# A hybrid decoder block on one core: B's Gram products and key transposes in a fixed order over both PSUM banks

## The chip, the core and the metric

The kernel runs on one core of a Trainium2 chip. The metric is the device time of one execution in microseconds (us). A core has several engines that work side by side, each through its own queue of instructions in order: TensorE (PE; it loads weights, PEld, and multiplies, PE), VectorE (DVE), ScalarE (ACT), GpSimd (POOL) and SyncE (SP), which here issues nearly all DMAs. PE writes its products into PSUM, which is divided into banks; DVE and ACT read them from there into SBUF, the working memory.

## What is computed

The input is 1024 tokens of width 1024, with 16 learned meta tokens put in front. One layer does three things: a half-step SwiGLU feed-forward, a pair of mixers whose outputs are gated and merged, and another half-step SwiGLU. The change lies in the mixers:

```python
u = _rmsnorm(h, mix_norm[l])
aq, ak, av, az, abeta, aalpha, bcols, ga, gb = jnp.split(u @ w_in[l], ...)
o_a = _deltanet_branch(aq, ak, av, az, abeta, aalpha, ...)   # A: chunked gated DeltaNet, 8 heads of 128
o_b = _rwkv7_branch(bcols, ...)                              # B: RWKV-7 time mixing, 16 heads of 64
merged = jax.nn.sigmoid(ga) * o_a + jax.nn.sigmoid(gb) * o_b
h = h + merged @ w_out[l]
```

Mixer B is a recurrence over tokens, for each head with a 64 x 64 state:

```python
def step(state, inp):
    r_t, w_t, k_t, v_t, a_t, b_t = inp
    sa = jnp.einsum('bhvk,bhk->bhv', state, a_t)
    state = state * w_t[:, :, None, :] + sa[..., None] * b_t[:, :, None, :] \
        + v_t[..., None] * k_t[:, :, None, :]
    return state, jnp.einsum('bhvk,bhk->bhv', state, r_t)
```

The kernel computes it in chunks of 64 tokens. Within a chunk it needs the products of the chunk's keys with its queries (the Gram products), the inverse of a triangular matrix made from them, and the keys transposed.

## The kernel before

**Stages.** The first feed-forward runs from 0 to about 730 us of the profiled execution, the mixers (`middle`) from there to about 2260 us, then the output projection and the second feed-forward. The tokens are in two segments: the first has 512 tokens and the 16 meta tokens, the second the other 512. `middle` runs 16 iterations, numbered 0 to 15: for each segment the eight values of `j`, and each iteration handles one head of A and two heads of B, which lie in the lower and the upper 64 partitions (`HS[0]`, `HS[1]`).

**Pipelining.** A list written out by hand (`schedule()`, with the strings `REGULAR`, `SWITCH` and others) says in which order the actions of neighbouring iterations are written: `merge_blocks` and `transitions` of the current iteration, then `operands` and `inverses` of the next one, `chains` and `gates` of the current, `finish`, then `decay`, `new_b` and `new_a` of the one after the next.

**What sets the order on an engine.** The functions write instructions, and a scheduler in the tile framework puts those of each engine into one fixed order when the kernel is built, by when it reckons that their inputs and their memory are ready, and else by the order in which they were written. It also sets the waits. So neighbouring instructions of the source may be far apart on PE, with instructions of other actions between them. `g.tc.issue_after(ins)` says that what is traced under it on the engine of `ins` comes somewhere behind `ins`. Before the change only `chains` uses it.

**PSUM.** In `middle` eight banks are shared out: two for `ch` (merge_blocks, transitions, chains), and for the rest `main_banks(g, 2, 2)` gives four to the projections (`pp`) and two to `mx`, from which all small products of `operands`, `new_b` and others come. At the step `banks`, near the end of the first segment, `main_banks(g, 1, 3)` makes that three and three.

**The Gram products (L1428).** `operands` takes the eight chunks of its two heads in two groups of four (`c4`). For each group it takes two `mx` tiles `ps[0]` and `ps[1]`, a bank each. For a chunk there are four products: `h` picks the lower or upper 64 partitions to read (64 rows of the array), `d` the bank, and `h ^ d` the 64 partitions of the bank that are written (64 columns of the array). Thus each of the four products of a chunk uses another quarter of the array: `d` = 0 the two quarters on the diagonal, into bank 0; `d` = 1 the other two, into bank 1. Each has 128 columns to stream. DVE then reads each bank, masks it and writes `LT` (L1431), bank 0 first.

**What follows from LT.** `inverse_inputs` sends the diagonal 32 x 32 blocks of LT to a buffer in HBM (`scr`) with eight DMAs on SP (L1548), then four of A's matrix `UA` (L1551), and reads it all back as `Ub` (L1557). `inverses` then runs 31 steps on DVE, two instructions each (`tb` L1581, `Xb` L1583), and its result comes back by DMA for the next iteration's `merge_blocks`. In `new_b` a product named `bon` (a sum over channels, L1213) follows a row of DVE instructions.

**The key transposes (L1498).** Further down in `operands`, two `mx` tiles `ps` take the transposed keys and b vectors of all eight chunks: again four products for a chunk, with `d` and `h` as above, here against an identity, 64 columns each. ACT copies both banks into `BKt` (L1501), which the next `transitions` needs.

Of the kernel before, what the change touches and what calls it, by code (L numbers as in the profile page):

```python
# [13 lines left out]
P = 128  # L14
# [12 lines left out]
CB = 64  # L27
# [6 lines left out]
HS = (slice(0, 64), slice(64, 128))  # L34
# [1018 lines left out]
def ch3(ap, c):  # L1053
    return ap.rearrange("p (a b) -> p a b", b=c)
# [189 lines left out]
def key(i, h):  # L1244

    return 1 - tok(i, h)


def run(g, pool, name, *kinds):


    ps, out, used = {}, [], [0, 0]
    for f in kinds:
        ds = [f(i, 0)[2] ^ f(i, 0)[3] for i in range(2)]
        at = []
        for d in ds:
            if d not in ps:
                ps[d] = pool.tile([P, 512], F32, name=name, tag=pool.name)
            at.append(used[d])
            used[d] += NCB // 2 * CB  # L1260
        for i in range(NCB):
            e, c0 = ds[i & 1], at[i & 1] + i // 2 * CB
            for h in range(2):
                l, r, src, dst = f(i, h)
                assert src ^ dst == e
                g.nc.tensor.matmul(ps[e][HS[dst], c0 : c0 + CB], lhsT=l, rhs=r, start=True, stop=True)  # L1266
        out.append([(ch3(ps[d][:, c0 : c0 + NCB // 2 * CB], CB), cs) for d, c0, cs in zip(ds, at, EO)])
    return out
# [50 lines left out]
def new_b(g, q):  # L1319
# [12 lines left out]
    for ps, cs in run(g, g.mx, "vbp", lambda i, h: (v[HS[h], off + i * CB : off + (i + 1) * CB],  # L1332
                                                    g.C("cmat")[HS[h], HS[h]], h, key(i, h)))[0]:
        nc.scalar.activation(Vs[:, cs], ps, AF.Copy)
# [76 lines left out]
def operands(g, q):  # L1411

    nc, st, V, c, j, n, off = g.nc, g.st, g.V, q.c, q.j, q.n, q.off
# [3 lines left out]
    kq, AR, BK = q.kq, q.AR, q.BK  # L1417
# [2 lines left out]


    LT = q.LT = st.tile([P, NCB, 2, P], F32, name="LT", tag="LT", bufs=2)
    for c4 in range(0, NCB, 4):
        ps = [g.mx.tile([P, 512], F32, name="grb", tag="mx") for _ in range(2)]
        for i in range(4):
            for d in range(2):
                for h in range(2):
                    nc.tensor.matmul(ps[d][HS[h ^ d], i * P : (i + 1) * P], lhsT=BK[HS[h], c4 + i, d ^ (i & 1)],  # L1428
                                     rhs=AR[HS[h], c4 + i].rearrange("p a b -> p (a b)"), start=True, stop=True)
        for d in range(2):  # L1430
            nc.vector.tensor_tensor(LT[:, c4 : c4 + 4, d], ch3(ps[d], P),  # L1431
                                    g.C("mB").unsqueeze(1).to_broadcast([P, 4, P]), op=ALU.mult)
    if meta:
        nc.vector.tensor_copy(g.bkpm[0:64, 0, :], g.bkm[0:64, :])
        nc.vector.tensor_copy(g.bkpm[64:128, 1, :], g.bkm[64:128, :])
        ps = g.mx.tile([P, 512], F32, name="gbm", tag="mx")
# [25 lines left out]
    for b in range(2):  # L1462
        ps = g.mx.tile([P, 512], F32, name="gra", tag="mx")
        for c2 in range(2):
            i = 2 * b + c2
            tsl = slice(off + i * CA, off + (i + 1) * CA)
            nc.tensor.matmul(ps[:, c2 * 256 : c2 * 256 + 256], lhsT=kq[:, 0, tsl], rhs=kq[:, :, tsl],  # L1467
                             start=True, stop=True)
# [23 lines left out]
    BKt = q.BKt = st.tile([P, NCB, 2, CB], F32, name="BKt", tag="BKt")  # L1492
    ident = g.C("ident")
    ps = [g.mx.tile([P, 512], F32, name="bkt", tag="mx") for _ in range(2)]
    for i in range(NCB):
        for d in range(2):
            for h in range(2):
                nc.tensor.matmul(ps[d][HS[h ^ d], i * CB : (i + 1) * CB], lhsT=BK[HS[h], i, d ^ (i & 1)],  # L1498
                                 rhs=ident[HS[h], HS[h]], start=True, stop=True)
    for d in range(2):  # L1500
        nc.scalar.activation(BKt[:, :, d], ch3(ps[d], CB), AF.Copy)  # L1501

# [4 lines left out]
    def vr(i, h):  # L1507
        k = key(i, h)
        return Vs[HS[k], i], LT[HS[k], i, 1 - (i & 1), CB:], k, h

    pa, pr = run(g, g.mx, "vp", lambda i, h: (AR[HS[h], i, 0, :], ident[HS[h], HS[h]], h, tok(i, h)), vr)
    for ps, cs in pa:
        nc.scalar.activation(at[:, cs], ps, AF.Copy)
    for ps, cs in pr:
        nc.scalar.activation(ch3(yb, CB)[:, cs], ps, AF.Copy)
    if meta:
        btm = q.btm = st.tile([64, P], F32, name="btm", tag="btm", bufs=2)
        ps = g.mx.tile([P, 512], F32, name="btp", tag="mx")
# [3 lines left out]
    ps = g.mx.tile([P, 512], F32, name="ktp", tag="mx")  # L1522
# [3 lines left out]
    if meta:  # L1526
        vkm = q.vkm
        ps = g.mx.tile([P, 512], F32, name="vmp", tag="mx")
# [11 lines left out]
def inverse_inputs(g, q):  # L1540
# [4 lines left out]
    for b in range(4):  # L1545
        sl, lo = slice(32 * b, 32 * b + 32), 32 * (b % 2)
        for e, cs in enumerate(EO):
            nc.sync.dma_start(sv[b][:, cs], q.LT[sl, cs, e, lo : lo + 32])  # L1548
    for b in range(4):
# [55 lines left out]
def merge_blocks(g, q):  # L1605

    nc, st = g.nc, g.st
    LT, UA, Xc, XA = q.LT, q.UA, q.Xc, g.XA
    Y = g.Y[q.it % 2]
# [3 lines left out]
    for t in range(NT):  # L1613
        for o in (0, 64):
            u12 = LT[o : o + 32, t, t & 1, 32:64] if t < NCB else UA[o : o + 32, t - NCB, o + 32 : o + 64]
            nc.tensor.matmul(ps[o + 32 : o + 64, t * 32 : t * 32 + 32], lhsT=u12, rhs=nat(Xc[o : o + 32, t]),
# [28 lines left out]
def transitions(g, q):  # L1645

    nc, st = g.nc, g.st
    Y = g.Y[q.it % 2]
    AR, LT, BKt, Vs, yb = q.AR, q.LT, q.BKt, q.Vs, ch3(q.yb, CB)
    vbk = q.vbk = st.tile([P, NCB, CB], F32, name="vbk", tag="vbk")  # L1650
# [20 lines left out]
    def vb(i, h):  # L1671
        k = key(i, h)
        return BKt[HS[k], i, 1 - (i & 1)], Vs[HS[k], i], k, h

    px, pv = run(g, g.ch, "xp", solved(q.at), va)
    for ps, cs in pv:
        nc.scalar.activation(vka[:, cs], ps, AF.Copy)
# [130 lines left out]
def finish(g, q):  # L1808
# [17 lines left out]
    else:  # L1826
        g.mg.append(u_tile(g, yb))


ACTIONS = {"new_b": new_b, "tokens": tokens, "new_a": new_a, "operands": operands, "inverses": inverses, "merge_blocks": merge_blocks, "transitions": transitions,  # L1830
           "chains": chains,
           "gates": gates, "finish": finish, "fill": fill}
# [86 lines left out]
```

## Time and profile before

| | |
|---|---|
| median of three runs | 3012.78 us (3006.31 to 3014.66) |
| profiled execution, its own time | 3009.62 us |
| its span, first to last instruction | 3007.6 us |
| PE busy | 2890.0 us (96%) |
| DVE busy | 2194.8 us (73%) |
| mean granted PE clock | 0.99 |
| busy on Gram products (L1428), 1024 records | 60.77 us of PE |
| busy on key transposes (L1498), 1024 records | 29.81 us of PE |

The profile is one execution. Its page has the busy time of each engine, the chain of work that ended last, and groups of instructions; the trace behind it answers by line, by window and as a timeline. A timeline row has the start and the length of a run of like instructions in us, engine, line, operation, output and inputs, shapes and the count, and in brackets how long the engine was idle before it and what ended that. A run's length goes to the end of its last instruction, and runs on PE overlap where products of different quarters do.

### The profile page before, as it was taken

The page shows a single profiled execution, that of the slowest core. Times are in us where ns is not written, and L with a number is a line of the kernel's source. Part 1 is how long each engine was busy: PE and PEld are TensorE (multiplying, and loading weights), DVE is VectorE, ACT ScalarE, POOL GpSimd, SP SyncE. Part 2 cuts the span into 40 slices and gives each one's busy share as a digit, 9 for nine tenths or more (in the row PEclk, how much of TensorE's full clock was granted, in tenths as well). Part 3 has the DMA queues.
Part 4 walks back from the last instruction along what each step waited for, and adds up shares of the span by engine and source line. Part 5 has one row for each costly group of instructions (what it writes and reads, how often), then busy time and mean ns, then how long its engine had stood idle before and what let it go on. Part 6 is the DMA issues. An engine that isn't in the chain of part 4 may idle for free.

```text
span 3007.6 us, 62829 instructions
## 1 busy us (share of the span) xinstructions
PE 2890.0 (96%) x25630; PEld 2501.7 (83%) x25630; DVE 2194.8 (73%) x4079; ACT 1445.0 (48%) x2546; POOL 491.2 (16%) x554
## 2 busy tenths in 40 slices
PE   8999999998989999999998999999998999999998
PEld 8999999998878888888776777777776888888886
DVE  7566668776667877788767887777866666667886
ACT  5322234345655656566566656656644432223444
POOL 0332332323000000000000100100100033332531
PEclk9999999999999999999999999999999999999999
DMA  3433236453232322333332332233354333333762
GB/s 123 134 107 106 93 122 210 170 193 111 74 74 66 83 72 64 81 82 87 93 90 71 81 82 75 74 84 86 106 148 158 114 109 103 100 104 132 248 226 95
DMA packets 286849, 333.14 MB, mean 111 GB/s; under 512 B 172432, under 2 KB 178576, under 8 KB 286560
## 3 DMA queue, kind: packets, MB, share of 16 engines
q1 hardware_dynamic: 284752, 325.77, 35.7%
q8 instruction: 201, 3.29, 0.5%
q10 hardware_dynamic: 1728, 3.16, 0.3%
q14 instruction: 88, 0.72, 0.1%
q0 software_dynamic: 80, 0.19, 0.0%
HBM read 261.67 MB, written 67.38 MB: 109 GB/s over the span
## 4 chain that ended last, share of the span: by engine, by line
PE 50%; DVE 12%; ACT 5%; issue 2%; DMA 1%; SPq 0%; POOL 0%; DVEq 0%; ACTq 0%
PE pp L307 16%; PE pg L494 11%; PE pd L707 6%; PE pwo L307 3%; DVE w L164 2%; DVE tb L1581 1%; PE pg L518 1%; DVE Xb L1583 1%; ACT w L163 1%; PE cs L1213 1%; PE vp L1266 1%; PE mp L1266 1%; DVE mt L1689 1%; PE gra L1467 1%; PE np L1266 1%
## 5 line engine op out<-in xcount | busy, mean ns | idle before, releaser
L307 PE MATMUL pp<-uk,w 128*128 128x512 f32 (+2 forms) x4824 | 969.8, 347 | 15.2 <-DVE h L714 6.0
L307 PEld LDWEIGHTS pp<-uk,w 128*128 128x128 f32 x4824 | 744.0, 191 | 111.9 <-DVE w L164 13.1
L707 PE MATMUL pd<-form,w 128*128 128x256 f32 (+2 forms) x2772 | 437.2, 320 | 9.9 <-DVE w L164 9.2
L707 PEld LDWEIGHTS pd<-form,w 128*128 128x128 f32 x2772 | 396.7, 190 | 49.9 <-DVE w L164 12.3
L494 PE MATMUL pg<-bt,w 128*128 128x256 f32 (+2 forms) x2520 | 401.7, 318 | 2.5 <-DVE w L164 2.0
L164 DVE TENSOR_TENSOR w<-wraw,w 128x1024 fp32r<-128x1024 f32 (+2 forms) x266 | 349.2, 1313 | 74.9 <-ACT w L163 71.8
L494 PEld LDWEIGHTS pg<-bt,w 128*128 128x128 f32 x2520 | 360.2, 188 | 36.4 <-DVE w L164 3.1
L163 ACT ACTIVATE w<-wraw 128x1024 fp32r<-128x1024 f32 (+2 forms) x266 | 276.5, 1040 | 191.5 <-PE pg L494 116.1
L500 DVE TENSOR_TENSOR c<-c,pg 128x520 f32<-128x520 f32 (+1 forms) x280 | 189.5, 689 | 240.0 <-PE pg L494 216.0
L494 PE MATMUL pg<-b,w 128*128 128x256 f32 (+2 forms) x2160 | 347.9, 318 | 0.0
L494 PEld LDWEIGHTS pg<-b,w 128*128 128x128 f32 x2160 | 309.8, 188 | 28.0
L163 ACT ACTIVATE w<-wrx 128x1024 fp32r<-128x1024 f32 (+1 forms) x64 | 58.4, 912 | 280.4 <-PE pg L494 238.5
L464 POOL TENSOR_TENSOR wrx<-wrx 128x512 f32<-128x512 f32 x38 | 52.5, 1382 | 727.0 <-DVE w22b L164 549.8
L164 DVE TENSOR_TENSOR form<-form 128x520 fp32r<-128x520 f32 (+1 forms) x152 | 145.1, 991 | 13.0 <-ACT form L163 12.7
L163 ACT ACTIVATE w<-wsum 128x768 fp32r<-128x768 f32 x96 | 75.7, 788 | 160.3 <-PE pd L707 120.9
L164 DVE TENSOR_TENSOR w<-wsum,w 128x768 fp32r<-128x768 f32 x96 | 116.0, 1214 | 36.8 <-ACT w L163 36.8
L1583 DVE TENSOR_TENSOR Xb<-Xb,tb 115x126 f32<-115x126 f32 (+22 forms) x496 | 125.8, 254 | 8.9 <-DVE tb L1581 0.2
L163 ACT ACTIVATE form<-form 128x520 fp32r<-128x520 f32 (+1 forms) x152 | 94.2, 632 | 77.1 <-DMA form<-frm 67.7
L1581 DVE TENSOR_TENSOR tb<-Ub,Xb 115x126 f32<-115x126 f32 (+22 forms) x496 | 124.5, 251 | 8.4 <-DMA Ub<-scr 1.2
L242 POOL TENSOR_TENSOR wsum<-wsum,wraw 128x768 f32<-128x768 f32 (+1 forms) x48 | 96.3, 2020 | 209.7 <-DMA wraw<-in_wdn 122.1
L1390 DVE SCALAR_TENSOR_TENSOR acc<-xr,pk,acc 128x528 f32<-128x528 f32 (+1 forms) x144 | 108.9, 757 | 28.5 <-ACT acc L1386 28.0
L307 PE MATMUL pwo<-uk,w 128*128 128x512 f32 x384 | 99.5, 412 | 4.1 <-DVE w L164 1.9
(424 smaller groups left out, 4391.3 us busy)
## 6 DMA issues: line engine op xcount, KB each, us to landing
wraw<-in_win SPq DMA_DIRECT2D x150, 512.0 KB
wraw<-in_wgu SPq DMA_DIRECT2D x44, 512.0 KB
wrx<-in_wgu SPq DMA_DIRECT2D x44, 512.0 KB
frm<-c SPq DMA_DIRECT2D x76, 260.0 KB
form<-frm SPq DMA_DIRECT2D x76, 260.0 KB
frm<-c SPq DMA_DIRECT2D x76, 256.0 KB
form<-frm SPq DMA_DIRECT2D x76, 256.0 KB
wraw<-in_wdn SPq DMA_DIRECT2D x40, 384.0 KB
```

The costliest lines, as they stand in the source:

```text
L163: g.nc.scalar.activation(hi, src, AF.Copy)
L164: (eng or g.nc.vector).tensor_tensor(lo, src, hi.bitcast(F32), op=ALU.subtract)
L242: g.nc.gpsimd.tensor_tensor(s, x, y, op=ALU.add if r == 1 else ALU.subtract)
L307: g.nc.tensor.matmul(ps, lhsT=l, rhs=r, start=i == 0, stop=i == n - 1)
L464: sums.tensor_tensor(a22, a21, a22, op=ALU.add)
L494: nc.tensor.matmul(ps[:, c0 : c0 + cn], lhsT=l[:, x, k, :], rhs=r[:, k, y, c0 : c0 + cn], start=i == 0, stop=i == 3 * HK - 1)
L500: nc.vector.tensor_tensor(o, x, y, op=ALU.add)
L707: nc.tensor.matmul(pd[:, c0 : c0 + cn], lhsT=wd[:, u, k - k0, :], rhs=x[:, v, c0 : c0 + cn], start=k + i == 0, stop=k == HF - 1 and i == 2)
L1266: g.nc.tensor.matmul(ps[e][HS[dst], c0 : c0 + CB], lhsT=l, rhs=r, start=True, stop=True)
L1390: nc.vector.scalar_tensor_tensor(acc[:, :n], xr[:, tap : tap + n], V("convw", ct * 4 + tap), acc[:, :n], op0=ALU.mult, op1=ALU.add)
L1581: nc.vector.tensor_tensor(tv, U[:, i, i + 1 :].unsqueeze(2).to_broadcast([npt, nt, ncc]), X[:, i, 0:ncc].unsqueeze(1).to_broadcast([npt, n ...
L1583: nc.vector.tensor_tensor(X[:, i + 1 :, 0:ncc], X[:, i + 1 :, 0:ncc], tv, op=ALU.add)
```

## The change

A helper `in_line` makes a function `mm` that issues a matmul and puts each behind the one that it issued before. The Gram products of an iteration and its key transposes each go through such a function. The loop over `d` is turned, so that for each chunk the two quarters of bank 1 come first and then the two of bank 0. The order is thus fixed: bank 1, rows 0 and 64, then bank 0, rows 0 and 64, chunk by chunk, and for the Gram products the second group behind the first. Other instructions may still stand between them. The products, their operands, the tiles and their reads are the same.

```diff
+def in_line(g):
+
+    last = []
+
+    def mm(ps, **kw):
+        with ExitStack() as behind:
+            if last:
+                behind.enter_context(g.tc.issue_after(last.pop().ins))
+            last.append(g.nc.tensor.matmul(ps, start=True, stop=True, **kw))
+
+    return mm
...
     LT = q.LT = st.tile([P, NCB, 2, P], F32, name="LT", tag="LT", bufs=2)
+    mm = in_line(g)
     for c4 in range(0, NCB, 4):
         ps = [g.mx.tile([P, 512], F32, name="grb", tag="mx") for _ in range(2)]
         for i in range(4):
-            for d in range(2):
+            for d in (1, 0):
                 for h in range(2):
-                    nc.tensor.matmul(ps[d][HS[h ^ d], i * P : (i + 1) * P], lhsT=BK[HS[h], c4 + i, d ^ (i & 1)],
-                                     rhs=AR[HS[h], c4 + i].rearrange("p a b -> p (a b)"), start=True, stop=True)
+                    mm(ps[d][HS[h ^ d], i * P : (i + 1) * P], lhsT=BK[HS[h], c4 + i, d ^ (i & 1)],
+                       rhs=AR[HS[h], c4 + i].rearrange("p a b -> p (a b)"))
...
     ps = [g.mx.tile([P, 512], F32, name="bkt", tag="mx") for _ in range(2)]
+    mm = in_line(g)
     for i in range(NCB):
-        for d in range(2):
+        for d in (1, 0):
             for h in range(2):
-                nc.tensor.matmul(ps[d][HS[h ^ d], i * CB : (i + 1) * CB], lhsT=BK[HS[h], i, d ^ (i & 1)],
-                                 rhs=ident[HS[h], HS[h]], start=True, stop=True)
+                mm(ps[d][HS[h ^ d], i * CB : (i + 1) * CB], lhsT=BK[HS[h], i, d ^ (i & 1)],
+                   rhs=ident[HS[h], HS[h]])
```

## The prediction

> **What bounds the kernel now.** I read the page's totals and its chain first, then the windows of one steady mixer iteration of each segment, then the waits of PE in the mixers.
>
> ```profile
> span 3007.6 us, 62829 instructions
> PE 2890.0 (96%) x25630; PEld 2501.7 (83%) x25630; DVE 2194.8 (73%) x4079; ACT 1445.0 (48%) x2546; POOL 491.2 (16%) x554
> PE 50%; DVE 12%; ACT 5%; issue 2%; DMA 1%; SPq 0%; POOL 0%; DVEq 0%; ACTq 0%
> 1139.00:1233.00 94.00, 90.82 (x1128) 78.95 (x1127) 72.89 (x182) 55.47 (x116) 4.51 (x22) 1.00 0.30 76
> 1814.00:1901.00 87.00, 83.71 (x942) 66.80 (x941) 70.38 (x167) 52.76 (x103) 7.92 (x15) 1.00 0.30 82
> PE bon L1213 <- ACT hl L163: 17.4, 12, 7.6
> 1217.68 0.50 PE L1213 MATMUL bon<-hl,bdr 128*128 128x512 f32 x1 [0.15 <-ACT hl L163]
> 1883.53 0.50 PE L1213 MATMUL bon<-hl,bdr 128*128 128x512 f32 x1 [1.49 <-ACT hl L163]
> ```
>
> PE is busy for 96% of the span and leads the chain. In the two window rows the columns are PE, PEld, DVE, ACT, POOL: an iteration of the first segment lasts 94 us and leaves PE 3.2 us, one of the second lasts 87 us and leaves it 3.3 us. They differ in one wait. `bon`, at the end of `new_b`, hangs on a line of DVE work: PE waits 0.15 us for it in the first segment, 1.49 us in the second, and 7.6 us once, at the change of segment. So the first segment is PE's, and the second has a stretch that is DVE's, in which PE time that is saved only makes a wait longer. The whole argument turns on that.
>
> **The change part by part.** It adds no instruction. Each of the 16 iterations has 32 Gram products (two groups of 16, L1428) and 32 key transposes (L1498). The groups of the trace:
>
> ```profile
> L1428 PE MATMUL grb<-AR,BK x1024: 266/270/470, 794.4 to 2174.5; 64*64 64x128 f32 x171
> L1498 PE MATMUL bkt<-ck,BK x1024: 217/218/268, 805.7 to 2182.2; 64*64 64x64 f32 x171
> 851.59 1.10 PE L1428 MATMUL grb<-AR,BK 64*64 64x128 f32 x32
> 794.36 1.47 PE L1428 MATMUL grb<-AR,BK 64*64 64x128 f32 x32
> 796.54 1.09 PE L1428 MATMUL grb<-AR,BK 64*64 64x128 f32 x16
> 798.21 1.09 PE L1428 MATMUL grb<-AR,BK 64*64 64x128 f32 x16 [0.57 <-DVE LT L1431]
> 853.75 1.55 PE L1428 MATMUL grb<-AR,BK 64*64 64x128 f32 x32
> ```
>
> 1024 records for 16 x 32 products are two records for each. A row's second number runs to the end of its last record (0.27 us), so the distance of starts in the 851.59 group is (1.10 - 0.27)/31 = 27 ns; in the 796.54 half it is (1.09 - 0.27)/15 = 55 ns. With records of 270 ns, that is two rates of one and the same work. The slow half is 16 records in a row, then a stop for DVE's read of a bank, then 16 more: one bank, which only two quarters of the array can write, after the other. The fast group has both banks mixed. So the bank-after-bank order costs twice the time, and the fixed order is worth the difference wherever the scheduler now chose it:
> - Gram, iteration 0: 1.47 - 1.10 = 0.4 us in the first group, 2 x 1.09 - 1.10 = 1.1 in the second.
> - Gram, iteration 1: 1.55 - 1.10 = 0.45 in the second group; its first is the fast one.
> - Gram later: groups lie in pieces between the products of `transitions` and fill its waits; taken as nothing. That cover is the waits for ACT's copies of `at` and `xv`; without it the pieces cost what is bounded below for a slipped group.
>
> The transposes:
>
> ```profile
> 1657.52 1.16 PE L1498 MATMUL bkt<-ck,BK 64*64 64x64 f32 x64
> 805.65 1.79 PE L1498 MATMUL bkt<-ck,BK 64*64 64x64 f32 x64
> 978.43 1.56 PE L1498 MATMUL bkt<-ck,BK 64*64 64x64 f32 x64
> 1449.43 1.55 PE L1498 MATMUL bkt<-ck,BK 64*64 64x64 f32 x64
> 1744.39 1.15 PE L1498 MATMUL bkt<-ck,BK 64*64 64x64 f32 x32
> 1746.58 0.97 PE L1498 MATMUL bkt<-ck,BK 64*64 64x64 f32 x26
> 2179.08 1.15 PE L1498 MATMUL bkt<-ck,BK 64*64 64x64 f32 x32
> 2181.27 0.97 PE L1498 MATMUL bkt<-ck,BK 64*64 64x64 f32 x26
> ```
>
> Best is iteration 9: 64 records in 1.16 us, (1.16 - 0.22)/63 = 15 ns apart. Iteration 0 took 1.79 (0.6 more). Iterations 2 to 7 (first and last shown) took 1.55 (0.4 more, six times: 2.4). Iterations 10 to 15 (first and last shown) take the banks 1.1 us apart, 1.15 + 0.97 = 2.1 us and six stragglers: 1.0 more, six times: 6.0. Iteration 1 is interleaved and iteration 8 lies ahead of the 7.6 us stop: nothing.
>
> PE time saved: 0.4 + 1.1 + 0.45 + 0.6 + 2.4 = 5 us in the first segment and 6 us in the second, 11 in all.
>
> Two rules of the Trainium skill speak against these terms. "TensorEngine Tiling (Array Packing)", section "Restrictions and Gotchas", says that different row tiles cannot access the same PSUM bank at once; here both quarters of a bank have different rows, so by that rule a bank takes one quarter at a time, 32 Gram records need 16 rounds where the fast row has 8, and the sum would be nothing. The 851.59 row disagrees. "TensorE: Matmul & The Clock Gate", section "Wait — 56ns, not 53.3ns?", says that starts never come closer than about 25 ns however few the columns; by it 64 transposes need 1.6 us and the first segment's transposes gain nothing. The 1657.52 row, at 15 ns, disagrees.
>
> **What reaches the end.** In the first segment nearly all: PE leads there and other products are always ready behind. What is added is a wait: a block begins with bank 1, the one that comes free later, so its first quarter waits for both. Behind it in PE's queue stand the projections `pp` and the state chain (`p`, `b`), and DVE and ACT wait for the latter. Where the scheduler puts a projection in front the wait costs nothing; where it misjudges, the nearest row is the 0.57 us of 798.21. I take -5 us for the segment; its bounds are -5 and, with that wait once in each of eight iterations, -5 + 8 x 0.57 = -0.4.
>
> The second segment:
>
> ```profile
> 1655.15 1.28 DVE L1431 TENSOR_TENSOR LT<-grb,ck 128x512 f32<-128x512 f32 x2
> 1664.55 0.78 SPq L1557 DMA_DIRECT2D Ub<-scr  x2
> 1668.59 0.19 DVE L1581 TENSOR_TENSOR tb<-Ub,Xb 115x31 f32<-115x31 f32 x1 [0.41 <-DMA Ub<-scr]
> 1741.59 1.28 DVE L1431 TENSOR_TENSOR LT<-grb,ck 128x512 f32<-128x512 f32 x2
> 1742.29 4.37 SPq L1548 DMA_DIRECT2D scr<-LT  x8
> 1746.76 2.91 SPq L1551 DMA_DIRECT2D scr<-UA  x4
> 1751.01 0.78 SPq L1557 DMA_DIRECT2D Ub<-scr  x2
> 1755.39 0.18 DVE L1581 TENSOR_TENSOR tb<-Ub,Xb 115x31 f32<-115x31 f32 x1
> 1160.50 1.28 DVE L1431 TENSOR_TENSOR LT<-grb,ck 128x512 f32<-128x512 f32 x2
> 1171.38 0.42 SPq L1557 DMA_DIRECT2D Ub<-scr  x1
> 1177.25 0.18 DVE L1581 TENSOR_TENSOR tb<-Ub,Xb 115x31 f32<-115x31 f32 x1
> ```
>
> The inverses (`tb`, `Xb`) start the DVE stretch that ends at `bon`. They need `Ub`, which comes through SP's queue: eight DMAs of LT as soon as its last group's first bank is read, four of UA, their landing, then `Ub`. In iteration 9 DVE stood 0.41 us waiting for `Ub`, 4.04 us after its issue; in iteration 10 it began 4.38 us after, 0.3 us of slack. Iteration 9 had the fast transposes: from their start to `tb` it took 1668.59 - 1657.52 = 11.07 us; with the slow ones 1755.39 - 1744.39 = 11.00. The second of slow order is thus hidden behind `Ub` already, and taking it out gave nothing there. Bounds: 0 and -6 us; I take 0, the row of iteration 9 being the thing itself. In the first segment the gap from issue to `tb` is 1177.25 - 1171.38 = 5.9 us, and nothing waits.
>
> Moved past queues: both banks of a group now end together, so ACT's two copies and DVE's two reads follow each other; in iteration 0 LT's first DMA on SP starts up to 1 us later. LT's order on SP stays. POOL is not touched.
>
> Sum: -5 us on the profiled execution's 3009.6 us (span 3007.6 and 2 us around it), 3004.6. That execution lies 3.2 us below the median of the three runs, 3012.8; on the median it is **3007.8, written 3008**.
>
> **The rivals.**
> - *Everything converts.* Less waiting in the chain `p` moves DVE's other work ahead of `Ub`, or LT comes earlier as well, and the 6 us of the second segment count: -11, 3002 us. For it: PE is 96% busy. Against it: the 1.49 us at `bon` in every iteration, and iteration 9.
> - *It does not do what it says.* An order among these products keeps nothing else out from between them: the scheduler may set projections between the bank 1 pair and the bank 0 pair, and the quarters still run two at a time. 0 to -2, 3012 us. The pieces in `transitions` show how readily it interleaves.
> - *LT's second group slips behind DVE's other work* (slower). In the second segment `Ub` has 0.3 us of slack, and LT's place in DVE's queue is the scheduler's choice:
>
> ```profile
> 1826.17 1.73 DVE L1689 TENSOR_TENSOR mt<-mp,ck 64x256 f32<-64x256 f32 x4 [1.35 <-PE mp L1266]
> 1827.91 0.76 DVE L1692 TENSOR_TENSOR AR<-mp,AR 128x256 f32<-128x256 f32 x2
> 1742.99 0.76 DVE L1695 TENSOR_TENSOR vbk<-np,vbk 128x256 f32<-128x256 f32 x2
> 1743.66 0.42 DVE L1698 TENSOR_TENSOR yb<-np,yb 128x256 f32<-128x256 f32 x1
> 1743.99 0.68 DVE L1696 TENSOR_TENSOR vbk<-vbk,gam 128x512 f32<-128x512 f32 x1
> ```
>
>  Now it stands behind `mt` and `AR` and ahead of `vbk` and `yb`. If both banks come free only after those, LT is 1742.99 to 1744.67 and a `yb` more, about 2.1 us, later, `Ub` with it, and seven iterations lose 7 x 2 = 14 us against 5 gained: +9, 3022 us. From 0.7 us of slip an iteration the gain is gone (7 x 0.7 = 5).
>
> **How the numbers follow.** My forecast 0.42; everything converts 0.30; no effect 0.12; LT slips 0.16. A measurement of this kernel tells about 0.3%, 9 us, from no change, and its three runs span 8 us. The second case, at -11, is past that bound in seven of ten: 0.21; my forecast's lower tail adds one in six, 0.07: faster 0.28. The slip at its full 2 us stands on the bound, and it may be longer or shorter: 0.10, and 0.04 from the upper tails of the others: slower 0.14. Within: 0.58. The range reaches down past the full saving by the spread of the runs, to 2996, and up to nearly the full slip, 3020.
>
> **What would show it.** Right: every row of the transposes x64 at about 1.16 us, none x32; the Gram groups of iterations 0 and 1 at 1.10; iterations of the first segment 93.5 us apart instead of 94, those of the second still 87; `bon`'s wait grown towards 2.4 us; `tb` still about 14 us after LT's second group. The forecast is wrong if iterations of the second segment shorten (everything converts) or LT's second read is found behind `vbk` (slip), and its first step is wrong if the transposes still come two at a time. A new order of the schedule at the change of segment, where 7.6 us lie open, would be outside all of this.

## The result, and the profile after

The changed kernel is a little slower. Over 20 runs each it takes 3012.7 us in the median against 3006.4 us before; the ratio is **1.0018, 95% interval [1.0009, 1.0026]**, some 5 us or 0.2%. The forecast was 5 us the other way. (The 3012.8 us of before, on which 3008 was built, were three runs; the ratio is what counts.)

The page of the changed kernel, its totals and its chain:

```profile
span 3012.5 us, 62862 instructions
PE 2887.3 (96%) x25630; PEld 2500.0 (83%) x25630; DVE 2194.4 (73%) x4079; ACT 1445.9 (48%) x2546; POOL 487.7 (16%) x554
PE 47%; DVE 11%; ACT 6%; DMA 3%; issue 2%; SPq 1%; POOL 0%; DVEq 0%; ACTq 0%; POOLq 0%
```

PE's busy time fell by 2.7 us, not by 11, while the span grew. Windows of one steady iteration of each segment, changed kernel (from the first `xp` product of `transitions` to the next iteration's; columns as before: us, then PE, PEld, DVE, ACT, POOL):

```profile
1155.10:1250.50 95.40, 91.27 (x1130) 78.69 (x1130) 73.16 (x181) 55.72 (x116) 4.24 (x22) 1.00 0.29 75
1912.36:1999.93 87.57, 83.53 (x945) 66.80 (x944) 70.28 (x166) 52.73 (x102) 8.22 (x15) 1.00 0.30 82
```

These are iterations 4 and 12, which took 94.0 and 86.9 us before: 1.4 and 0.7 us less. In the means of the table further down it is 1.3 and 0.8. The waits at `bon` of the changed kernel, in the view of PE's waits (us in total, times, longest) and in the timeline:

```profile
PE bon L1213 <- ACT hl L163: 9.3, 9, 1.5
```

```profile
1131.75 0.51 PE L1213 MATMUL bon<-hl,bdr 128*128 128x512 f32 x1
1889.83 0.50 PE L1213 MATMUL bon<-hl,bdr 128*128 128x512 f32 x1 [1.49 <-ACT hl L163]
```

The wait in the second segment is the 1.49 us it was: PE has won nothing that could stand there. The 7.6 us at the change of segment are down to two waits of 0.9.

What became of the transposes shows in the timelines of iteration 4, on PE, ACT and DVE. Before:

```profile
1167.35 1.55 PE L1498 MATMUL bkt<-ck,BK 64*64 64x64 f32 x64
1168.83 0.49 PE L1739 MATMUL p<-SA,kq 128*128 128x128 f32 x2
1168.87 1.09 ACT L1501 ACTIVATE BKt<-bkt 128x512 f32<-128x512 f32 x2 [2.30 <-PE bkt L1498]
1169.36 0.29 DVE L1741 TENSOR_TENSOR rhA<-Va,p 128x128 f32<-128x128 f32 x1 [1.48 <-PE p L1739]
1169.70 0.93 PE L1266 MATMUL vp<-ck,AR 64*64 64x64 f32 x30
```

After (all products of the change now carry the helper's line, L1257):

```profile
1175.44 0.33 PE L1257 MATMUL bkt<-ck,BK 64*64 64x64 f32 x4
1175.70 0.96 PE L307 MATMUL pp<-uk,w 128*128 128x512 f32 x3
1176.47 0.60 ACT L1135 ACTIVATE gs<-pp 128x512 f32<-128x512 f32 x1 [1.82 <-PE pp L307]
1176.59 1.15 PE L1257 MATMUL bkt<-ck,BK 64*64 64x64 f32 x60
1176.97 1.05 ACT L163 ACTIVATE w<-wraw 128x1024 fp32r<-128x1024 f32 x1
1177.67 0.49 PE L1754 MATMUL p<-SA,kq 128*128 128x128 f32 x2
1178.05 1.23 DVE L164 TENSOR_TENSOR w<-wraw,w 128x1024 fp32r<-128x1024 f32 x1 [2.08 <-ACT w L163]
1179.11 1.06 ACT L1516 ACTIVATE BKt<-bkt 128x512 f32<-128x512 f32 x2
1179.19 0.28 DVE L1756 TENSOR_TENSOR rhA<-Va,p 128x128 f32<-128x128 f32 x1
1179.74 1.11 PE L1279 MATMUL vp<-ck,AR 64*64 64x64 f32 x30 [0.65 <-ACT BKt L1516]
```

Read the two from the block's start. The transposes are as dense as promised, (1.15 - 0.22)/59 = 16 ns apart. But the block is **split**: bank 1's first pair of products, then three projections, then the rest, which ends 2.3 us after the start instead of 1.55. The three projections let ACT go on with a gate (`gs`) and with the next weights (`w`), and DVE with its share of `w`; these stand ahead of the copies of `BKt` and of `rhA`, a step of the state chain. ACT starts on `BKt` 3.67 us after the block's start (before 1.52), DVE on `rhA` 3.75 (before 2.01), and PE waits 0.65 us for `BKt`. Iterations 3 to 7 all have this split; in iteration 2 two products `am` and two projections stand in the gap. In the second segment the block is split as well: in iterations 10 to 15 two `p`, two `b` and five projections stand between x4 and x60.

In the second segment the place to look at is DVE. Changed kernel, timeline of DVE, iterations 10, 12 and 13:

```profile
1740.85 0.69 DVE L1445 TENSOR_TENSOR LT<-grb,ck 128x512 f32<-128x512 f32 x1 [0.30 <-PE grb L1257]
1747.04 1.88 DVE L1445 TENSOR_TENSOR LT<-grb,ck 128x512 f32<-128x512 f32 x3
...
1936.36 0.19 DVE L1596 TENSOR_TENSOR tb<-Ub,Xb 115x31 f32<-115x31 f32 x1 [0.65 <-DMA Ub<-scr]
1936.47 1.23 DVE L164 TENSOR_TENSOR w<-wraw,w 128x1024 fp32r<-128x1024 f32 x1
...
2024.01 0.19 DVE L1596 TENSOR_TENSOR tb<-Ub,Xb 115x31 f32<-115x31 f32 x1 [0.45 <-DMA Ub<-scr]
```

Before, DVE read the four Gram banks two and two (1741.59 x2 in the prediction). Now it reads one, then the other three together behind `mt` and `AR`. The last read comes 10.8 us after the iteration's first `xp` product, 10.2 before: 0.6 us late. `Ub` follows through its DMAs, and DVE, whose next instruction is `tb`, stands idle for it: 0.45 to 1.32 us in each of iterations 10 to 15. Before, in iterations 10 to 13, it did not. In iterations 10 to 14 `tb` starts 0.3 to 1.1 us later after `xp` than before, and each iteration is longer by the same amount to 0.12 us (iteration 14: 1.12 and 1.16). So the late `tb` is what the second segment loses.

### The profile page after: what moved, and what is told of

Same layout as the page of the kernel before. It is cut to its first block, busy times and chain, and to the rows that moved or that the text cites. A ratio compares the mean times of both kernels' runs of the same rounds, so it can differ in the third digit from the quotient of the medians.

```text
span 3012.5 us, 62862 instructions
## 1 busy us (share of the span) xinstructions
PE 2887.3 (96%) x25630; PEld 2500.0 (83%) x25630; DVE 2194.4 (73%) x4079; ACT 1445.9 (48%) x2546; POOL 487.7 (16%) x554
## 4 chain that ended last, share of the span: by engine, by line
PE 47%; DVE 11%; ACT 6%; DMA 3%; issue 2%; SPq 1%; POOL 0%; DVEq 0%; ACTq 0%; POOLq 0%
PE pp L307 16%; PE pg L494 11%; PE pd L707 5%; PE pwo L307 3%; DVE w L164 2%; ACT w L163 1%; PE pg L518 1%; DVE tb L1596 1%; DVE Xb L1598 1%; PE cs L1213 1%; PE mp L1279 1%; DMA Ub<-scr 1%; PE vp L1279 1%; PE xp L1279 1%; DVE mt L1704 1%
```

## The experiments

The kernels came in three sets, each timed beside its own runs of the kernel before. Iteration k in the table goes from the first `xp` product of the iteration ahead to its own; the middle goes from the first `bon` to the last iteration's `xp`. All are distances of starts in the profiled execution, in us. The last column is the timed ratio to before.

| run | mean, 3 to 6 | mean, 11 to 14 | sum, 7 to 9 | middle | ratio, 95% interval |
|---|---|---|---|---|---|
| before | 94.05 | 86.9 | 302.9 | 1481.0 | |
| changed | 95.35 | 87.7 | 296.3 | 1486.8 | 1.0018 [1.0009, 1.0026] |
| gram_only | 94.8 | 87.3 | 292.7 | 1482.8 | 1.0006 [0.9992, 1.002] |
| bkt_only | 95.3 | 86.5 | 298.1 | 1483.8 | 1.0006 [0.9993, 1.002] |
| d01 | 95.3 | 86.6 | 298.0 | 1484.9 | 1.0008 [0.9995, 1.0021] |
| loop_only | 94.1 | 87.1 | 300.8 | 1480.2 | 1.0014 [0.9996, 1.0031] |
| split_only | 95.3 | 86.6 | 301.1 | 1483.8 | 1.0 [0.9988, 1.0012] |
| half_line | 94.4 | 87.0 | 304.0 | 1487.2 | 1.0012 [0.9998, 1.0026] |
| seg2_bkt | 94.05 | 86.5 | 305.2 | 1481.4 | 0.9984 [0.9971, 0.9997] |
| best2 | 94.05 | 86.9 | 300.4 | 1476.1 | 0.998 [0.997, 0.9991] |
| late_bkt | 94.1 | 86.55 | 302.6 | 1482.3 | 0.9987 [0.9977, 0.9998] |
| gram_turn | 94.1 | 87.1 | 300.9 | 1479.5 | one run |

The timed ratios mostly cannot tell these kernels from before; the iterations can, since within a run those of one column mostly agree to 0.1 or 0.2 us. Wider are iterations 3 to 6 of gram_only (94.25 to 95.1) and iterations 11 to 14 of the changed kernel (87.5 to 88.1), half_line (86.5 to 87.5) and best2 (86.4 to 87.75).

**One half of the change at a time.** Edits against the changed kernel: *gram_only* gives the transposes their old loop and plain matmul back, *bkt_only* does so for the Gram products.

```diff
 # gram_only
     for i in range(NCB):
-        for d in (1, 0):
+        for d in range(2):
             for h in range(2):
-                mm(ps[d][HS[h ^ d], i * CB : (i + 1) * CB], lhsT=BK[HS[h], i, d ^ (i & 1)],
-                   rhs=ident[HS[h], HS[h]])
+                nc.tensor.matmul(ps[d][HS[h ^ d], i * CB : (i + 1) * CB], lhsT=BK[HS[h], i, d ^ (i & 1)],
+                                 rhs=ident[HS[h], HS[h]], start=True, stop=True)
```

> The fixed order on the Gram products alone; the key transposes go bank after bank as before. Theory A (two separate costs: the split transpose block makes each iteration of the first segment 1.3 us longer, the later second Gram group each of the second segment 0.6 us): iterations 3 to 6 take 94.0 us as before, iterations 10 to 14 take 87.5 us, transposes x64 in one piece in the first segment; ratio about 1.000 (0.6 x 7 = 4 us lost, about 4 us won at iterations 7 to 9). Theory B (the Gram order alone sets both, since the transposes stand behind it): iterations 3 to 6 at 95.3, ratio about 1.002. Theory C (the loss is a new order of the rest of the schedule, not tied to one block): neither 94.0 nor 95.3, ratio anywhere from 0.998 to 1.004.

> The fixed order on the key transposes alone; the Gram products go bank after bank as before. Theory A: iterations 3 to 6 take 95.3 us with x4 of the transposes ahead of three projections and x60 behind them, iterations 10 to 14 take 86.9 us or 0.1 to 0.3 less; ratio about 1.002 (1.3 x 6 = 8 us lost, some of it won back at iterations 7 to 9). Theory B: iterations 3 to 6 at 94.0 or a little below (the transposes' 0.4 us each is won), ratio 0.998 to 1.000. Theory C: neither.

The line on the transposes alone brings the whole 95.3 of the first segment, with x4 and x60 around three projections (theory A). In the second segment it gains 0.4 us. The line on the Gram products alone leaves the transposes whole, x64; 87.3 is near the 87.5 of theory A, but its 94.8 in the first segment is what theory C said, neither 94.0 nor 95.3: here the reads of `LT` come earlier (the last one 13.3 us after `xp`, not 14.1), and `bon` waits 0.5 to 0.8 us. So theory A holds for the transposes and not for the Gram products, and the two halves do not add up.

**The turn of the loop and the line apart.** *d01* keeps both lines but has `for d in (0, 1)`; *loop_only* keeps `for d in (1, 0)` and issues plain matmuls; *gram_turn* is the kernel before with only the Gram loop turned.

```diff
 # gram_turn, against before
-            for d in range(2):
+            for d in (1, 0):
                 for h in range(2):
                     nc.tensor.matmul(ps[d][HS[h ^ d], i * P : (i + 1) * P], lhsT=BK[HS[h], c4 + i, d ^ (i & 1)],
```

> The fixed order on both, but bank 0's pair ahead of bank 1's. Theory A with its cause in the line (the first pair goes when its own bank is free, the rest only when the other is): if bank 0's tile gets its bank last, the first pair waits for both, the block goes whole, and iterations 3 to 6 fall to 94.0 or 93.5, ratio 0.998 to 0.999; if bank 0's tile gets its bank first, the block is split all the same, iterations 3 to 6 at 95.3, ratio about 1.002. Theory D (the turn of the loop does nothing): the same times as the changed kernel in every iteration.

> The loops turned (bank 1's pair ahead of bank 0's in the text), but no instruction held behind another. Theory A (the line does it): iterations as before, 94.0 and 86.9, transposes x64 in one piece, ratio 0.999 to 1.001. Theory D (the order of the two banks in the text does it): iterations 3 to 6 at 95.3, ratio about 1.002.

> The kernel before, with only the Gram loop turned: bank 1's products ahead of bank 0's in the text, nothing held behind anything, transposes as before. If the turn alone makes the second Gram group late: the last LT product of iterations 10 to 14 comes 0.6 us later after the first Xp product than before (10.8 against 10.2), iterations 11 to 14 at 87.1 to 87.4 against 86.9, iterations 3 to 6 at 94.0 to 94.1. If it needs the line as well: 10.2 and 86.9. One look, so that the whole time says little.

The transposes of iteration 4 in d01, then in loop_only:

```profile
1172.20 0.33 PE L1257 MATMUL bkt<-ck,BK 64*64 64x64 f32 x4
1173.36 1.15 PE L1257 MATMUL bkt<-ck,BK 64*64 64x64 f32 x60
```

```profile
1166.91 1.56 PE L1513 MATMUL bkt<-ck,BK 64*64 64x64 f32 x64
```

With either pair first the transposes are split, and without the line they are whole, so the line does it and not the turn. The turn does the other thing. In the timeline of DVE of gram_turn, iteration 10:

```profile
1736.43 0.69 DVE L1431 TENSOR_TENSOR LT<-grb,ck 128x512 f32<-128x512 f32 x1 [0.30 <-PE grb L1428]
1742.63 1.88 DVE L1431 TENSOR_TENSOR LT<-grb,ck 128x512 f32<-128x512 f32 x3
```

One read and then three, the last 10.8 us after `xp`, as in the changed kernel, without any line; in d01 it is two and two and 10.2 us. So the turned Gram loop makes LT late. Alone it costs 0.2 us an iteration (87.1 against 86.9, in loop_only too). The whole change costs more than that turn less the 0.4 us of the line: only in the changed kernel does DVE wait for `Ub` in every iteration of the second segment; in gram_turn and bkt_only it does not in iterations 11 to 14. Two things come together there. `Ub` is issued later: in iteration 12 its first DMA goes out 20.2 us after `xp`, against 19.2 before and 19.6 in gram_turn and in bkt_only. And DVE has nothing left to do ahead of `tb`. Before and in gram_turn a step named `SA`, which waits for PE, comes last before `tb`. In bkt_only it is the step `w`, which prepares weights, in iteration 12:

```profile
1937.26 1.22 DVE L164 TENSOR_TENSOR w<-wraw,w 128x1024 fp32r<-128x1024 f32 x1
1938.39 0.18 DVE L1596 TENSOR_TENSOR tb<-Ub,Xb 115x31 f32<-115x31 f32 x1
```

In the changed kernel `w` and `SA` stand behind `tb` (1936.47 above), so that DVE stands idle until `Ub` is there and does them afterwards. What delays `Ub` beyond the 0.6 us of LT is not shown.

**The split without the four quarters.** *split_only*, against before: the transposes in line, but bank after bank with only bank 1's first pair ahead.

```diff
+    mm = in_line(g)
+    for i, d in [(0, 1)] + [(i, 0) for i in range(NCB)] + [(i, 1) for i in range(1, NCB)]:
+        for h in range(2):
+            mm(ps[d][HS[h ^ d], i * CB : (i + 1) * CB], lhsT=BK[HS[h], i, d ^ (i & 1)],
+               rhs=ident[HS[h], HS[h]])
```

> The kernel before, with all transposes in line, but bank after bank: bank 1's first pair, then the whole of bank 0, then the rest of bank 1. It has the split without the four quarters in turn. If the split (a pair, projections, the rest) is what costs: iterations 3 to 6 at 95.3 or up to 0.5 more, since the x60 come 23 to 25 ns apart and not 15. If the order over the four quarters itself costs something: 94.0. In the second segment: 86.5 if the earlier pair and what moves with it wins there, 86.9 to 87.0 if it is the denser transposes that win.

Its timeline in iteration 4:

```profile
1171.13 0.33 PE L1257 MATMUL bkt<-ck,BK 64*64 64x64 f32 x4
1171.39 0.96 PE L307 MATMUL pp<-uk,w 128*128 128x512 f32 x3
1172.28 1.79 PE L1257 MATMUL bkt<-ck,BK 64*64 64x64 f32 x60
1172.66 1.05 ACT L163 ACTIVATE w<-wraw 128x1024 fp32r<-128x1024 f32 x1
1173.74 1.23 DVE L164 TENSOR_TENSOR w<-wraw,w 128x1024 fp32r<-128x1024 f32 x1 [2.08 <-ACT w L163]
```

The x60 take 1.79 us here and 1.15 in bkt_only, and the iteration is 95.3 us in both. So the split sets the loss, and in this pair **the 0.6 us that the four quarters save reach nothing**. The pair is not alike in all else: `rhA` starts 5.72 us after the block in split_only and 3.76 in bkt_only. The windows of that iteration, first split_only, then bkt_only:

```profile
1150.81:1246.07 95.26, 92.11 (x1131) 79.63 (x1130) 73.47 (x181) 56.09 (x116) 5.23 (x22) 1.00 0.30 75
```

```profile
1156.13:1251.41 95.28, 91.50 (x1130) 78.71 (x1128) 73.11 (x181) 55.82 (x116) 4.50 (x22) 1.00 0.30 75
```

PE is busy 0.6 us less and idle 0.6 us more. In the second segment split_only has 86.6 and bkt_only 86.5: the denser order is worth 0.1 us there, and the other 0.3 come with the split. The 0.1 us is no more than the iterations of one run differ by. Where the rest comes from shows in the windows before and after `bon` of iteration 12, for the projections `pp` alone (PE's busy time and count first). Before, then split_only:

```profile
1906.04:1970.39 64.35, 39.15 (x148) 26.75 (x148) 2.93 (x4) 4.40 (x7) 1.00 0.32 79
1970.39:1992.90 22.51, 17.23 (x68) 12.55 (x68) 0.00 (x0) 3.01 (x5) 1.00 0.33 91
```

```profile
1911.08:1975.42 64.34, 39.33 (x149) 26.98 (x149) 2.92 (x4) 4.41 (x7) 1.00 0.28 73
1975.42:1997.71 22.29, 17.06 (x67) 12.35 (x67) 0.00 (x0) 3.01 (x5) 1.00 0.36 110
```

The stretch up to `bon` takes the same time, set by DVE; one projection more is done in it, and one fewer (0.22 us) is left for the stretch behind, which is PE's. That `tb` starts 1 us later than before (24.4 us after `xp`, not 23.4) costs nothing, since the `w` of DVE shown above for bkt_only is done ahead of `tb` and no longer between `tb` and `bon`.

**A later second bank.** *half_line*, its edit against split_only: half of bank 0 first, so that the second bank is asked for after sixteen records and not after four.

```diff
-    for i, d in [(0, 1)] + [(i, 0) for i in range(NCB)] + [(i, 1) for i in range(1, NCB)]:
+    for i, d in [(i, 0) for i in range(4)] + [x for i in range(4) for x in ((i, 1), (i + 4, 0))] + [(i, 1) for i in range(4, NCB)]:
```

> The kernel before, with all transposes in line, half of bank 0 ahead, then the two banks in turn, then the second half of bank 1: the second bank is asked for 0.4 us later. In the first segment the schedule sets one projection between x16 and x48 in place of three between x4 and x60. If the projections in between set the loss: iterations 3 to 6 fall from 95.3 most of the way to 94.0, to 94.0 to 94.5. If any line on the transposes costs the first segment 1.3 us: 95.3. Ratio 0.998 to 1.000 in the first case, 1.001 to 1.002 in the second.

Its timeline in iteration 4:

```profile
1174.41 0.68 PE L1257 MATMUL bkt<-ck,BK 64*64 64x64 f32 x16
1175.02 0.50 PE L307 MATMUL pp<-uk,w 128*128 128x512 f32 x1
1175.45 1.15 PE L1257 MATMUL bkt<-ck,BK 64*64 64x64 f32 x48
1176.21 1.09 ACT L1514 ACTIVATE BKt<-bkt 128x512 f32<-128x512 f32 x2 [2.60 <-PE bkt L1257]
1177.06 0.29 DVE L1754 TENSOR_TENSOR rhA<-Va,p 128x128 f32<-128x128 f32 x1 [2.12 <-PE p L1752]
1180.83 1.05 ACT L163 ACTIVATE w<-wraw 128x1024 fp32r<-128x1024 f32 x1
```

The block ends 2.19 us after its start, hardly earlier than the changed kernel's 2.30. But with one projection in between no weights slip in front: ACT's `w` starts 6.4 us after the block's start, not 1.5, and `rhA` 2.65, not 3.75. The iteration takes 94.4 us: two thirds of the 1.3 us are back. So it is mostly what was let in ahead, and little the later end of the transposes. Whether the early weights on ACT and DVE or the late chain is the dearer part was not separated. A late `rhA` alone does not set the price: it starts 5.72 us after the block in split_only and 3.75 in the changed kernel, and both iterations take 95.3 to 95.4 us; both have the early `w`. The scheduler is taken to split the block because the second bank comes free later than the first; half_line fits that, but no run shows it. As a whole the kernel is no better than before. In the second segment two of its four iterations take 87.3 to 87.5 us: there `tb` waits 1.3 us for `Ub`, which is issued 20.2 and 20.4 us after `xp`; in the two that take 86.5 to 86.6 us it is issued 18.5 and 18.8 us after `xp`, and `tb` does not wait.

**What is worth keeping.** *seg2_bkt* is the kernel before with the transposes in line, bank 0's pair first, under `if not meta`, which is the second segment; *late_bkt* has `if q.it >= 10` in its place; *best2* is seg2_bkt with the Gram products of iterations 8 and 9 in line too, bank 1's pair first.

```diff
+    if not meta:
+        mm = in_line(g)
+        for i, d in [(i, d) for i in range(NCB) for d in (0, 1)]:
+            for h in range(2):
+                mm(ps[d][HS[h ^ d], i * CB : (i + 1) * CB], lhsT=BK[HS[h], i, d ^ (i & 1)],
+                   rhs=ident[HS[h], HS[h]])
+    else:
...
 # best2, in addition
+        if q.it in (8, 9):
+            mm = in_line(g) if c4 == 0 else mm
+            for i in range(4):
+                for d in (1, 0):
...
```

> The kernel before, with the transposes of the second segment alone put in line (bank 0's pair ahead of bank 1's); Gram products and the first segment's transposes as before. Theory A (the +1.3 us of the first segment comes from the split of its transposes, and what the line wins lies in the second segment): iterations 3 to 6 at 94.0, iterations 11 to 14 at 86.5, iteration 9 at about 83; from the first Xp product of iteration 6 to that of iteration 15 812 to 814 us against 819.7; ratio 0.997 to 0.998. Rival (what the second segment won in the run of the transposes alone depends on how the first one was ordered): iterations 11 to 14 at 86.9, ratio 0.999 to 1.001.

> As the run with the second segment's transposes in line, and with the Gram products of iterations 8 and 9 in line as well, bank 1's pair first. In the run with the Gram products alone iteration 9 took 79.95 us, against 82.9 with the transposes in line and 86.5 before. If that is won in iteration 9 itself: 3 us less than the run with the second segment's transposes alone, ratio 0.996 to 0.997. If it was only moved there from the first segment: the same time as that run or up to 3 us more.

> The kernel before, with the transposes of iterations 10 to 15 alone in line (bank 0's pair first). It leaves the change of segment (iterations 7 to 9) as the kernel before has it. If the 0.35 us an iteration of the second segment are won there and not carried in from the change of segment: iterations 11 to 14 at 86.5 to 86.6, iterations 7 to 9 together at 302.9 as before, the stretch from iteration 6 to iteration 15 about 3 us shorter than 819.7; ratio 0.999. If the gain hangs on the changed iterations 8 and 9: 86.9 and 819.7.

The 86.5 us of the second segment come without any change in the first, and late_bkt shows that they are not carried in from the change of segment: iterations 7 to 9 take 302.6 us there, and the gain begins at iteration 10. From iteration 6 to 15 it is 816.5 us against 819.7, the 3 us expected. By their timed ratios late_bkt, seg2_bkt and best2 (**0.998 [0.997, 0.9991]**) are 0.1 to 0.2% faster than before, which is 0.2% faster than the changed kernel. For late_bkt the 2.9 us of iterations 10 to 15 are about what is timed. seg2_bkt wins the same 2.9 us there, but iteration 8 grew from 85.7 to 92.7 us and 9 shrank from 86.5 to 81.9, so that from iteration 6 to 15 it takes 819.1 us, not the 812 to 814 expected. Its profiled execution is the slowest of its twelve (3012.1 us, median 3003.4), and does not explain its timed gain. In best2 iteration 9 (81.35 us) did not reach the 80 of gram_only, and it is timed like seg2_bkt. Its iterations 7 to 9 are together 2.5 us shorter than before, but 1.9 of these stand in iteration 7, where the granted clock was 1.00 against 0.99 before; and 1.4 us of its shorter middle stand in iteration 1, where the code is the same and the clock was 0.98 against 0.94. By its profile the edit itself wins 0.7 us in iterations 8 and 9 and 1.5 in iterations 10 to 15.

## Why the prediction was wrong

**The rates were right.** With both banks in turn 60 transposes stand 16 ns apart, forecast 15. The first Gram group of iteration 0, in PE's timeline of the changed kernel:

```profile
798.73 1.09 PE L1257 MATMUL grb<-AR,BK 64*64 64x128 f32 x28
```

That is (1.09 - 0.27)/27 = 30 ns, forecast 27. The Gram groups were split as well: this one has x4 and a projection ahead of it, and in the second group of iteration 0 the first x4 waited 1.40 us for DVE's read of a bank, where the forecast's bound took 0.57.

The Trainium skill, "TensorEngine Tiling (Array Packing)", section "Restrictions and Gotchas", says that different row tiles cannot access the same PSUM bank at once. The forecast set the 27 ns of the fast row against it, but by this rule bank after bank is one quarter at a time and both banks in turn are two, so that the step from 55 to 27 ns alone would fit it. What speaks against it is the length of one record: records of 128 columns on the whole array (`vap`) start 0.11 us apart in the kernel before, in the median. If a quarter needs as long, one quarter at work in each bank would give starts some 55 ns apart, an estimate from that figure, and the 30 ns disagree. The Trainium skill, "TensorE: Matmul & The Clock Gate", section "Wait — 56ns, not 53.3ns?", says that starts never come closer than about 25 ns. The 16 ns disagree.

**The first step that failed: "Where the scheduler puts a projection in front the wait costs nothing".** Three projections went between the first pair and the rest in iterations 3 to 7, and iterations 3 to 6 took 1.3 us more each. The price was worked out for a wait (0.57 us at most) and for PE's time (a projection is work that has to be done), and what a projection lets loose on ACT and DVE was put at nothing. The bound of -0.4 us for the segment was too good by the whole sum of the splits, 4 x 1.3 = 5.2 us in iterations 3 to 6 alone. The rival "it does not do what it says" had the insertion, but only as a lost gain, 0 to -2 us; the sign "the transposes still come two at a time" would not have found it, since the block is split and dense at once.

**The second: "In the first segment nearly all: PE leads there".** The 95.3 us of the split iteration were the same with 0.6 us of PE time saved (bkt_only) and without (split_only). A wait of 0.15 us at `bon` and 97% busy do not show that a saving on PE arrives. Whether the saving would arrive in a block that is whole was not tried: no version here had transposes both dense and whole in the first segment.

**The second segment.** That the dense transposes would give nothing was right to 0.1 us. The reason given, `Ub`, was only half of it: in the runs with the line and the old Gram order `tb` starts later than before without waiting for `Ub`, and the iteration is shorter nonetheless, since one more projection is done under cover of DVE's stretch. The third rival, **LT slips**, is what happened in the changed kernel: 0.6 us of slip where 0.3 us of slack was read, just under the 0.7 at which it was to eat the gain; iterations 10 to 15 lost 4.1 us together. Its place was not behind `vbk` and `yb`, though, but the second read of the first group, behind `mt` and `AR`; and its cause was the turn of the loop, which the forecast had not priced by itself.

**Outside the sum.** Iterations 7 to 9 won 6.6 us. A new order at the change of segment was named as possible and not priced. The windows of the three, before and then after:

```profile
1429.11:1731.99 302.88, 283.01 (x2969) 223.11 (x2967) 234.89 (x547) 183.34 (x349) 22.43 (x51) 0.98 0.32 84
```

```profile
1441.11:1737.43 296.32, 281.44 (x2968) 223.57 (x2967) 232.94 (x547) 183.99 (x349) 19.84 (x51) 0.98 0.33 86
```

PE's idle time fell from 302.88 - 283.01 = 19.9 us to 14.9. Over the runs this stretch takes 292.7 to 305.2 us. Iteration 7 goes with the granted clock: it takes 127.9 to 128.9 us in the eight runs that had 1.00 there, 130.5 to 130.7 in the three with 0.99 (before is one of them), and 131.8 in half_line with 0.97. Whether the order of the instructions makes the clock fall there is not shown. That leaves some 4.7 us won in iterations 8 and 9, for which I found no rule.

The account of the middle, +5.8 us: iterations 3 to 6 +5.2, iterations 7 to 9 -6.6, iterations 10 to 15 +4.1, and +3.1 before iteration 3. The last cannot be laid to the change: late_bkt, which is the kernel before up to iteration 10, took 4.3 us longer there than the profiled run of before. It too goes with the clock. The windows from the first `bon` to the first `xp`, before, then late_bkt (the third number from the end is the clock):

```profile
767.78:877.42 109.64, 99.91 (x971) 86.60 (x971) 76.30 (x179) 63.05 (x119) 8.09 (x23) 0.98 0.28 73
```

```profile
768.77:882.68 113.91, 104.03 (x972) 90.35 (x973) 76.43 (x179) 63.10 (x119) 8.04 (x23) 0.94 0.26 71
```

The changed kernel took 114.55 us there, at 0.94. Without that stretch and iterations 1 and 7, whose clock differs as well, +0.7 (iteration 2) + 5.2 - 4.7 + 4.1 = +5.3 us are left, about what was timed. So the size of the result is partly luck: the splits and the late `Ub` lost 10 us, and 4.7 were won where nothing had been forecast.

## What to carry to other kernels

An order among a block's own instructions does not keep the block together: if the first may start before the last has its bank, a scheduler may put other work in the gap, and that work's consumers on other engines come with it. Price an inserted instruction by what it releases, not by its own length. Turning a loop that writes two buffers also turns which buffer is done first; look who reads them, and in which order. And before a difference between two profiles is laid to an edit, compare the granted clock of the same stretch, and a stretch that the edit does not touch.

## What was not expected of the hardware

Nothing in the engines' rates. The granted clock differed between executions of the same code: 0.98 before and 0.94 in late_bkt between the first `bon` and the first `xp`, where late_bkt took 4.3 us longer. What the runs showed besides is how far the parts fall short of adding up: the turn of the Gram loop costs 0.2 us an iteration of the second segment, the line on the transposes gains 0.4, and the two lines with the turn lose 0.8 (87.7 against 86.9).
